# Regrouping the activations of a gated recurrence: the last three gates and the softplus exponential around the first gelu product

## The chip, the cores and the metric

The kernel runs on one core of a Trainium2 chip. The metric is the device time of one execution in microseconds (us). The engines that matter here are TensorE (PE, matrix products), VectorE (DVE, elementwise work, here also the scans), ScalarE (ACT, activation functions and copies with a scale) and SyncE (SP, which issues the loads). Each engine works through its own queue in order; the engines wait for each other through semaphores.

## The reference

One hybrid block over 16 meta tokens and 512 input tokens (528 rows of width 1024): a gated linear recurrence (RG-LRU) beside a retention branch, mixed, and then a convolutional feed-forward. The change touches the recurrence branch and, behind it, meets the projections of the retention branch:

```python
xr = causal_dwconv(u_rnn, rnn_conv_w, rnn_conv_b)
r = sigmoid(xb @ w_a + b_a)              # 10 blocks of 128 channels
i = sigmoid(xb @ w_x + b_x)
log_a = -8 * r * softplus(-lam)
a = exp(log_a)
b = sqrt(-expm1(2 * log_a)) * (i * x)
h_t = a_t * h_{t-1} + b_t                # scan over the tokens
o_a = h * gelu(u_gate)
...
q = rotary(xn @ w_q); k = rotary(xn @ w_k) / 16     # 4 heads of 256
```

## The kernel before, in words

**Data and tiles.** Tokens lie along the free axis, 128 channels on the partitions. Every fp32 operand of a large product is split in two fp16 parts, high (by ACT) and low (by DVE), and a product is the sum of three fp16 products: high·high, high·low, low·high (`SPLIT`, in that order of weight and input). The helper `split` (L92 on ACT, L93 on DVE) does this for weights and inputs alike. `project` (L401) makes one 128-channel product: eight steps of 128 input channels, in each step three fp16 products over two column halves, so 48 matmuls. In each step the low part of the weight is used last.

**Weights.** The weights come in numbered units of 1 MB (`unit`), 256 columns by 1024 input channels. SyncE loads a unit into one of two raw buffers (`raw`), in the order of the units; a load therefore waits until the split of the unit two before it is done. A unit of the plain kind is split in two halves, input channels 0 to 511 and 512 to 1023, so that the first half serves steps 1 to 4 of a product and the second half steps 5 to 8. One call of `tick` emits the split of one such half, as long as the tiles split but still ahead of the unit in use stay within `ahead`, here 6 tiles or three units. One unit serves two products. The units run on in this order: five for the recurrence input (`u_ur`), five for its gelu gate (`u_ug`), then query and key of each retention head in turn (`u_q[0]`, `u_k[0]`, `u_q[1]`, ...).

**Accumulators.** In the stage here `acc` gives out four PSUM tiles of two banks; a new product takes a free one and otherwise waits until the reader of an earlier one is done.

**Order.** Up to `order.close()` the program fixes the order on PE, ACT and DVE by hand: each of the three issues exactly in the order in which the program states its instructions. SyncE is left to the framework's planner. Behind `order.close()` everything is placed by the planner, which runs a model of the engines and at each moment issues the ready instruction with the highest priority (the earlier stated, the higher). It may also set instructions stated behind `order.close()` between those of the hand-written order, but cannot change that order itself.

**The recurrence.** For each of the ten blocks n the first loop makes the input product (`conv_product`), the convolution taps (`conv_taps`, L611 and L613) and the split `xs` of the result. Three blocks later (`LAG = 3`) `rnn_gates` makes the two gate projections (six matmuls each) and their sigmoids on ACT (L630), then multiplies the input gate in on DVE (L632). So blocks 7, 8 and 9 are still without gates when the first loop ends. Then the softplus of `lam` is worked out on ten columns: an absolute value and an exponential on ACT (L677, L678) and a short polynomial on DVE (L676 to L692), which ends in the scales `cneg` and `cpos`.

The second loop makes the ten products of the gelu branch. Round n is: the product (PE), one `tick` (one half of a weight, on ACT and DVE), the gelu on ACT (L702), in the first three rounds the gates of block 7 + n, and then what `SPREAD` lists for the round, for five blocks at once: `rnn_tanh` (ACT, L635), `rnn_decay` (exponential on ACT, L639, and two DVE instructions, L641 and L642), `rnn_scan` (square root on ACT, L646, a multiply and a scan on DVE, L647 and L648). Before, tanh stands in rounds 2 and 4, decay in 3 and 5, scan in 7 and 9. ACT evaluates its functions from a table that holds one set of them at a time; a function of another set brings an `ACT_TABLE_LOAD`. Abs, copy and identity bring none.

**Behind it.** `rotary` makes the two products of a query or key head (L401), whose weight halves are the ones split by the last ticks, and turns them on DVE (L742 to L744), with the tables `rope` that SyncE loads (L723). `branch_a` multiplies gelu and scan (L715).

Of the kernel before, what the change touches and what calls it, by code (L numbers as in the profile page):

```python
# [8 lines left out]
F32 = mybir.dt.float32  # L9
F16 = mybir.dt.float16  # L10
AF = mybir.ActivationFunctionType
ORDERED = {mybir.EngineType.PE, mybir.EngineType.Activation, mybir.EngineType.DVE}
ALU = mybir.AluOpType

P = 128
# [6 lines left out]
NR = DR // P  # L22
# [4 lines left out]
TQ = T - T0  # L27
# [3 lines left out]
SW = 2.0 ** 8  # L31
S_XN = 4.0
S_XR = 4.0
# [18 lines left out]
def hybrid_block_kernel(ctx, tc, x, meta, norm_mix_g, w_in, conv_w, conv_b, rg_a_w, rg_a_b,  # L52
                        rg_x_w, rg_x_b, lam, w_brnn, w_bret, w_out, norm_ffn_g, w_up,
                        fconv_w, fconv_b, w_down, norm_final_g, rope_t, decay_t, out):
    nc = tc.nc
    const = ctx.enter_context(tc.tile_pool(name="const", bufs=1))
# [17 lines left out]
    def acc(name):  # L74
        return psum["acc"].tile([P, 2, 512], F32, name=name, tag="acc")
# [9 lines left out]
    def piece(shape, dtype, name):  # L85
        return pieces.tile(shape, dtype, name=name, tag="s")

    def wtile(name):
        return work.tile([P, T], F32, name=name, tag="w")
# [198 lines left out]
    def get(u):  # L288
        current[0] = max(current[0], u)
        while len(loaded) <= u:  # L290
            queue(unit_load())
        while done[0] < len(steps) and steps[done[0]][0] <= u:
            emit_step()
        return wviews[u]

    def tick(n=1):

        for _ in range(n):
            if done[0] == len(steps):
                if len(loaded) == len(units):  # L300
                    return
                queue(unit_load())
            u = steps[done[0]][0]
            if sum(unit_tiles(i) for i in range(current[0], u + 1)) > ahead[0]:
                return
            emit_step()
# [10 lines left out]
    vt1 = const.tile([P, P], F32, name="vt1")  # L317
# [72 lines left out]
    def x_of(hi, lo):  # L390
        tv = (hi, lo)
        return lambda a, k, c0, n: tv[a][:, k, c0:c0 + n]
# [3 lines left out]
    def project(ps, w, col, src, halves, nk):  # L396

        for k in range(nk):
            for aw, ax in SPLIT:
                for hf, (c0, n) in enumerate(halves):  # L400
                    nc.tensor.matmul(ps[:, hf, :n], w(aw, k, col, P), src(ax, k, c0, n),  # L401
                                     start=k == 0 and (aw, ax) == (0, 0), stop=k == nk - 1 and aw == 1)
# [173 lines left out]
    half_r, half_t, half_x, gate_g = {}, {}, {}, {}  # L576

    def part(hv, n):
        if n not in hv:
            hv[n] = piece([P, T], F32, "rnn")  # L580
        return hv[n]
# [17 lines left out]
    def conv_product(n):  # L599
        u, col = u_ur[n]  # L600
        if n in early:
            ps = early.pop(n)
            project_half(ps, get(u), col, xf, HR, 1)
        else:
            ps = acc("ps")
            project(ps, get(u), col, xf, HR, KD)
        return ps
# [8 lines left out]
    def conv_split(n):  # L616
        xs = work.tile([P, 2, 1, T], F16, name="xs", tag="w")
        split(xs[:, 0, 0], xs[:, 1, 0], part(half_x, n), S_XR)
        xr_split[n] = xs

    def rnn_gates(n):
        xs = xr_split.pop(n)
        xr = part(half_x, n)
        gi = wtile("gi")
        for nm, bias, dst in (("a", b_a, part(half_r, n)), ("x", b_x, gi)):
            ps = acc("ps")
            wt = gw[nm][0][n // 4]
            project(ps, lambda a, k, c0, m: wt[:, a, n % 4 * P:n % 4 * P + P], 0, x_of(xs[:, 0], xs[:, 1]),
                    [(0, 264), (264, 264)], 1)
            nc.scalar.activation(dst.rearrange("p (a b) -> p a b", a=2), ps[:, :, :264], AF.Sigmoid,  # L630
                                 scale=1.0 / (SW * S_XR), bias=bias[:, n:n + 1])
        nc.vector.tensor_mul(xr, xr, gi)  # L632

    def rnn_tanh(n):
        nc.scalar.activation(part(half_t, n), part(half_r, n), AF.Tanh, scale=cpos[:, n:n + 1])  # L635
# [14 lines left out]
    LAG = 3  # L650
# [3 lines left out]
    for n in range(NR):  # L654
        ps = conv_product(n)
        if n == 0:
            split_gates("a")
        if n >= LAG:
            tick(2 if n in (4, 6, 8) else 1)
            rnn_gates(n - LAG)  # L660
        conv_taps(n, ps)
        if n == 0:
            conv_split(0)
        if n == 1:
            split_gates("x")
        if n == 2:
            tick()
            conv_split(1)
            psum_layout(acc=4)
        if n >= 2:  # L670
            conv_split(n)


    lv = vt1[:, 70:80]
    sp = const.tile([P, 8, NR], F32, name="sp")
    nc.vector.tensor_scalar(sp[:, 0], lv, -1.0, 0.0, op0=ALU.mult, op1=ALU.max)  # L676
    nc.scalar.activation(sp[:, 1], lv, AF.Abs)  # L677
    nc.scalar.activation(sp[:, 2], sp[:, 1], AF.Exp, scale=-1.0)  # L678
    nc.vector.tensor_scalar_add(sp[:, 3], sp[:, 2], 2.0)
    nc.vector.reciprocal(sp[:, 4], sp[:, 3])  # L680
    nc.vector.tensor_mul(sp[:, 4], sp[:, 4], sp[:, 2])
    nc.vector.tensor_mul(sp[:, 5], sp[:, 4], sp[:, 4])
    nc.vector.memset(sp[:, 6], 1.0 / 15.0)
    for m in (13, 11, 9, 7, 5, 3, 1):
        nc.vector.tensor_mul(sp[:, 6], sp[:, 6], sp[:, 5])
        nc.vector.tensor_scalar_add(sp[:, 6], sp[:, 6], 1.0 / m)
    nc.vector.tensor_mul(sp[:, 6], sp[:, 6], sp[:, 4])
    nc.vector.scalar_tensor_tensor(sp[:, 7], sp[:, 6], 2.0, sp[:, 0], op0=ALU.mult, op1=ALU.add)
    cneg = const.tile([P, NR], F32, name="cneg")
    cpos = const.tile([P, NR], F32, name="cpos")  # L690
    nc.vector.tensor_scalar_mul(cneg, sp[:, 7], -8.0)
    nc.vector.tensor_scalar_mul(cpos, sp[:, 7], 8.0)  # L692


    ahead[0] = 6
    SPREAD = ((rnn_tanh, 2, 0), (rnn_decay, 3, 0), (rnn_tanh, 4, 5), (rnn_decay, 5, 5), (rnn_scan, 7, 0), (rnn_scan, 9, 5))
    for n in range(NR):
        ps = acc("ps")
        u, col = u_ug[n // 2], (n % 2) * P
        project(ps, get(u), col, xf, HQ, KD)  # L700
        tick()
        nc.scalar.activation(part(gate_g, n)[:, :TQ].rearrange("p (a b) -> p a b", a=2), ps[:, :, :257],  # L702
                             AF.Gelu_apprx_tanh, scale=1.0 / (SW * S_XN))
        if n < LAG:
            rnn_gates(NR - LAG + n)
        for f, n0, m0 in SPREAD:
            if n == n0:
                for i in range(m0, m0 + 5):
                    f(i)
# [357 lines left out]
    def branch(us, src, nk):  # L1067
        ps = acc("pm")
        project(ps, get(us.pop(0)), 0, src, HH, nk)
        tick(2)  # L1070
        return ps[:, :, :257]
# [26 lines left out]
    for i in range(2):  # L1098
# [5 lines left out]
        ps = branch(u_ba, oa_of, NR)  # L1104
# [525 lines left out]
```

## Time and profile before

| | |
|---|---|
| Median of 3 runs | 1068.04 us (1067.8 to 1068.93) |
| The profiled execution's own time | 1068.13 us |
| Its span in the profile | 1066.4 us |
| PE busy | 1049.7 us (98%) |
| PE weight loads (PEld) busy | 851.7 us (80%) |
| DVE busy | 860.2 us (81%) |
| ACT busy | 589.1 us (55%) |
| Granted TensorE clock | 0.999 |

The profile is of one execution, with times from the start of its span; 1.7 us of the execution's own time lie outside the span. A row of a timeline gives start, duration, engine, line and operation, what is written and read with its shape, and the number of merged instructions; in brackets how long the engine was idle before it, and what released it. A row of a list of waits gives the total, the number of waits and the longest. L12 is line 12 of the kernel; as `split` and `project` are helpers, many groups share lines 92, 93 and 401, and are told apart by their tiles. The stage of the second loop lies between about 81 and 139 us, the products of the first query head behind it up to 149.5, those of the first key head up to about 160.6.

### The profile page before, as it was taken

The page shows a single profiled execution, that of the slowest core. Times are in us where ns is not written, and L with a number is a line of the kernel's source. Part 1 is how long each engine was busy: PE and PEld are TensorE (multiplying, and loading weights), DVE is VectorE, ACT ScalarE, POOL GpSimd, SP SyncE. Part 2 cuts the span into 40 slices and gives each one's busy share as a digit, 9 for nine tenths or more (in the row PEclk, how much of TensorE's full clock was granted, in tenths as well). Part 3 has the DMA queues.
Part 4 walks back from the last instruction along what each step waited for, and adds up shares of the span by engine and source line. Part 5 has one row for each costly group of instructions (what it writes and reads, how often), then busy time and mean ns, then how long its engine had stood idle before and what let it go on. Part 6 is the DMA issues. An engine that isn't in the chain of part 4 may idle for free.

```text
span 1066.4 us, 21008 instructions
## 1 busy us (share of the span) xinstructions
PE 1049.7 (98%) x8995; PEld 851.7 (80%) x8995; DVE 860.2 (81%) x1289; ACT 589.1 (55%) x927; POOL 6.9 (1%) x20
## 2 busy tenths in 40 slices
PE   9999999999999999999999999999999999999997
PEld 6888888865684848888888886588888888888884
DVE  6885799998786969887787886479989897988975
ACT  8568954434564747566454453366566465454442
POOL 2000000000000000000000000000000000000000
PEclk9999999999999999999999999999999999999999
DMA  8331243431211322333333365032432324214322
GB/s 255 102 133 45 80 139 119 160 120 40 78 43 47 113 65 65 115 94 109 115 110 115 105 221 179 1 119 80 159 111 88 120 81 136 64 60 137 102 80 80
DMA packets 108989, 111.49 MB, mean 105 GB/s; under 512 B 5610, under 2 KB 100560, under 8 KB 108896
## 3 DMA queue, kind: packets, MB, share of 16 engines
q1 hardware_dynamic: 108448, 109.74, 32.0%
q8 instruction: 70, 1.15, 0.4%
q10 hardware_dynamic: 160, 0.27, 0.1%
q0 software_dynamic: 288, 0.14, 0.1%
q14 instruction: 23, 0.19, 0.1%
HBM read 108.04 MB, written 2.10 MB: 103 GB/s over the span
## 4 chain that ended last, share of the span: by engine, by line
PE 78%; DVE 14%; ACT 6%; issue 2%; ACTq 0%; DVEq 0%
PE ps L401 31%; PE P L1466 9%; PE pa L852 9%; PE pm L401 4%; PE ps L915 4%; PE ps L1189 4%; PE pe L852 4%; DVE wt L93 3%; PE ps L414 3%; PE pb L852 2%; PE pa L1353 2%; ACT wt L92 2%; PE ps L937 1%; DVE rnn L648 1%; PE pe L1353 1%
## 5 line engine op out<-in xcount | busy, mean ns | idle before, releaser
L401 PEld LDWEIGHTS <-wt 128*128 128x128 f16 x3840 | 373.2, 97 | 58.2 <-DVE t L742 1.4
L93 DVE SCALAR_TENSOR_TENSOR wt<-raw,wt 128x1024 f16<-128x1024 f32 (+2 forms) x278 | 303.9, 1105 | 64.9 <-ACT wt L92 63.6
L92 ACT ACTIVATE wt<-raw 128x1024 f16<-128x1024 f32 (+2 forms) x278 | 263.4, 962 | 151.3 <-PE P L1466 25.3
L852 PEld LDWEIGHTS <-wt 128*128 128x128 f16 x2016 | 195.0, 97 | 34.7 <-issue 7.4
L401 PE MATMUL ps<-x2h,wt 128*128 128x258 f16 x1184 | 181.2, 273 | 0.0
L401 PE MATMUL ps<-xh,wt 128*128 128x257 f16 (+2 forms) x1056 | 163.8, 275 | 1.1 <-DVE t L742 1.1
L401 PE MATMUL ps<-x2l,wt 128*128 128x258 f16 x592 | 113.2, 272 | 0.0
L401 PE MATMUL ps<-xl,wt 128*128 128x257 f16 (+2 forms) x528 | 102.2, 275 | 0.0
L1466 PE MATMUL P<-wt,act 128*128 128x256 f16 x792 | 88.3, 273 | 0.0
L1466 PEld LDWEIGHTS <-act 128*128 128x128 f16 x792 | 77.5, 98 | 9.0
L915 PE MATMUL ps<-wt,xh 128*128 128x512 f16 x256 | 76.1, 379 | 2.3 <-DVE v L93 2.3
L1331 DVE SCALAR_TENSOR_TENSOR cv<-ps,vt,cv 128x512 f32<-128x512 f32 x80 | 59.7, 747 | 22.8 <-ACT cv L1329 21.9
L852 PE MATMUL pa<-xs,wt 128*128 128x257 f16 x576 | 71.6, 273 | 3.4 <-ACT kept L857 3.1
L401 PE MATMUL pm<-oa,wt 128*128 128x257 f16 x480 | 55.4, 274 | 0.0
L1329 ACT ACTIVATE cv<-ps,vt,vt 128x512 f32<-128x512 f32 x40 | 31.0, 774 | 34.5 <-PE ps L401 33.8
L915 PEld LDWEIGHTS <-xh 128*128 128x128 f16 x256 | 24.8, 98 | 31.4 <-issue 3.4
L915 PE MATMUL ps<-wt,xl 128*128 128x512 f16 x128 | 48.3, 379 | 0.0
L256 DVE TENSOR_TENSOR raw<-raw 128x1024 f32<-128x1024 f32 x39 | 47.6, 1220 | 0.7
L852 PE MATMUL pa<-ob,wt 128*128 128x257 f16 x384 | 45.7, 274 | 0.6 <-ACT last L857 0.5
L1189 PE MATMUL ps<-wt,mx 128*128 128x512 f16 x192 | 44.3, 378 | 0.0
L1353 PEld LDWEIGHTS <-wt 128*128 128x128 f16 x336 | 32.6, 97 | 4.4
L1189 PEld LDWEIGHTS <-mx 128*128 128x128 f16 x192 | 17.7, 98 | 18.4
(290 smaller groups left out, 1417.1 us busy)
## 6 DMA issues: line engine op xcount, KB each, us to landing
raw<-in_w_in SPq DMA_DIRECT2D x40, 1024.0 KB, 4.9
raw<-in_w_up SPq DMA_DIRECT2D x24, 1024.0 KB, 5.2
raw<-in_w_down SPq DMA_DIRECT2D x48, 256.0 KB, 3.5
raw<-in_w_branch_ret SPq DMA_DIRECT2D x16, 512.0 KB, 4.5
raw<-in_w_branch_rnn SPq DMA_DIRECT2D x8, 640.0 KB, 4.6
raw<-in_w_out SPq DMA_DIRECT2D x4, 1024.0 KB, 4.9
xin<-in_x SPq DMA_DIRECT2D x4, 512.0 KB, 5.5
raw<-in_w_in SPq DMA_DIRECT2D x4, 512.0 KB, 8.1
```

Source lines behind the costliest of these rows:

```text
L92: a = nc.scalar.activation(hi, src, AF.Copy, scale=s)
L93: b = nc.vector.scalar_tensor_tensor(lo, src, s, hi, op0=ALU.mult, op1=ALU.subtract)
L256: nc.vector.tensor_tensor(pair, pair, rv[:, :, right].rearrange("p (h k) c -> p h k c", h=2), op=ALU.add)
L401: nc.tensor.matmul(ps[:, hf, :n], w(aw, k, col, P), src(ax, k, c0, n), start=k == 0 and (aw, ax) == (0, 0), stop=k == nk - 1 and aw == 1)
L414: mm = nc.tensor.matmul(ps[:, hf, :n], w(aw, k, col, P), src(ax, k, c0, n), start=k == 0 and (aw, ax) == (0, 0), stop=k == KD - 1 and aw == 1)
L852: nc.tensor.matmul(ps[:, :257], ws[k // 4](wf, aw, k % 4), src(xf_, ax, k), start=first and k == 0 and (aw, ax) == (0, 0), stop=k == last_ ...
L915: nc.tensor.matmul(pb, xf(ax, k, XF + j0, nb), w(aw, k % 4, 0, 512), start=i == 0, stop=i == 23)
L1189: nc.tensor.matmul(ps[:, n], mx[k][:, a, c0:c0 + P], wo[k // 2](aw, k % 2, n * 512, 512), start=k == 0 and (a, aw) == (0, 0), stop=k == ks ...
L1329: nc.scalar.activation(vv_, src[:, :, 2:258], AF.Identity, scale=vt2[:, 96 + ch:97 + ch], bias=bias)
L1331: nc.vector.scalar_tensor_tensor(vv_, src[:, :, j:j + 256], vt2[:, 48 * j + ch:48 * j + ch + 1], vv_, op0=ALU.mult, op1=ALU.add)
L1353: nc.tensor.matmul(ps[:, :258], w(wf, aw, k), x2_form(xf_, ax, k), start=first and k == 0 and (aw, ax) == (0, 0), stop=k == 3 and aw == 1, ...
L1466: nc.tensor.matmul(pd[:, 256 * tt:256 * tt + 256], t[:, ax, c0 + tt * P:c0 + tt * P + P], w(wf, aw, i), start=q % 6 == 0 and tt == 0 and i ...
```

## The change

The gates of blocks 7, 8 and 9 are all stated in round 0, behind the product and the tick and ahead of its gelu. Behind them comes the softplus (now in a function `decay_scales`, unchanged inside), then the gelu of round 0. The gelus are also tied behind the last gate's sigmoid on ACT's queue (`tc.issue_after`), and so is the softplus' work on ACT. The two scan groups move from rounds 7 and 9 to 6 and 8.

```diff
@@ rnn_gates
-            nc.scalar.activation(dst.rearrange("p (a b) -> p a b", a=2), ps[:, :, :264], AF.Sigmoid,
-                                 scale=1.0 / (SW * S_XR), bias=bias[:, n:n + 1])
+            a = nc.scalar.activation(dst.rearrange("p (a b) -> p a b", a=2), ps[:, :, :264], AF.Sigmoid,
+                                     scale=1.0 / (SW * S_XR), bias=bias[:, n:n + 1])
         nc.vector.tensor_mul(xr, xr, gi)
+        return a.ins
...
+    def decay_scales():
         lv = vt1[:, 70:80]
         sp = const.tile([P, 8, NR], F32, name="sp")
...
         nc.vector.tensor_scalar_mul(cneg, sp[:, 7], -8.0)
         nc.vector.tensor_scalar_mul(cpos, sp[:, 7], 8.0)
+        return cneg, cpos

     ahead[0] = 6
-    SPREAD = ((rnn_tanh, 2, 0), (rnn_decay, 3, 0), (rnn_tanh, 4, 5), (rnn_decay, 5, 5), (rnn_scan, 7, 0), (rnn_scan, 9, 5))
+    SPREAD = ((rnn_tanh, 2, 0), (rnn_decay, 3, 0), (rnn_tanh, 4, 5), (rnn_decay, 5, 5), (rnn_scan, 6, 0), (rnn_scan, 8, 5))
     for n in range(NR):
         ps = acc("ps")
         u, col = u_ug[n // 2], (n % 2) * P
         project(ps, get(u), col, xf, HQ, KD)
         tick()
-        nc.scalar.activation(part(gate_g, n)[:, :TQ].rearrange("p (a b) -> p a b", a=2), ps[:, :, :257],
-                             AF.Gelu_apprx_tanh, scale=1.0 / (SW * S_XN))
-        if n < LAG:
-            rnn_gates(NR - LAG + n)
+        if n == 0:
+            for i in range(NR - LAG, NR):
+                gates_done = rnn_gates(i)
+            with tc.issue_after(gates_done):
+                cneg, cpos = decay_scales()
+        with tc.issue_after(gates_done):
+            nc.scalar.activation(part(gate_g, n)[:, :TQ].rearrange("p (a b) -> p a b", a=2), ps[:, :, :257],
+                                 AF.Gelu_apprx_tanh, scale=1.0 / (SW * S_XN))
         for f, n0, m0 in SPREAD:
             if n == n0:
                 for i in range(m0, m0 + 5):
                     f(i)
```

More of the change, by code (lines that the diff above doesn't have):

```diff
@@ L671, in hybrid_block_kernel @@
             conv_split(n)
[L674 to L691, printed above, removed]
@@ L692, in hybrid_block_kernel @@
-    nc.vector.tensor_scalar_mul(cpos, sp[:, 7], 8.0)
+    def decay_scales():
+        lv = vt1[:, 70:80]
+        sp = const.tile([P, 8, NR], F32, name="sp")
+        nc.vector.tensor_scalar(sp[:, 0], lv, -1.0, 0.0, op0=ALU.mult, op1=ALU.max)
+        nc.scalar.activation(sp[:, 1], lv, AF.Abs)
+        nc.scalar.activation(sp[:, 2], sp[:, 1], AF.Exp, scale=-1.0)
+        nc.vector.tensor_scalar_add(sp[:, 3], sp[:, 2], 2.0)
+        nc.vector.reciprocal(sp[:, 4], sp[:, 3])
+        nc.vector.tensor_mul(sp[:, 4], sp[:, 4], sp[:, 2])
+        nc.vector.tensor_mul(sp[:, 5], sp[:, 4], sp[:, 4])
+        nc.vector.memset(sp[:, 6], 1.0 / 15.0)
+        for m in (13, 11, 9, 7, 5, 3, 1):
+            nc.vector.tensor_mul(sp[:, 6], sp[:, 6], sp[:, 5])
+            nc.vector.tensor_scalar_add(sp[:, 6], sp[:, 6], 1.0 / m)
+        nc.vector.tensor_mul(sp[:, 6], sp[:, 6], sp[:, 4])
+        nc.vector.scalar_tensor_tensor(sp[:, 7], sp[:, 6], 2.0, sp[:, 0], op0=ALU.mult, op1=ALU.add)
+        cneg = const.tile([P, NR], F32, name="cneg")
+        cpos = const.tile([P, NR], F32, name="cpos")
+        nc.vector.tensor_scalar_mul(cneg, sp[:, 7], -8.0)
+        nc.vector.tensor_scalar_mul(cpos, sp[:, 7], 8.0)
+        return cneg, cpos
```

## The prediction

> **What bounds the kernel now.** I read the busy shares first, then what TensorE waits for, then the window of the changed stage engine by engine, then the chain that ended last.
>
> ```profile
> PE 1049.7 (98%) x8995; PEld 851.7 (80%) x8995; DVE 860.2 (81%) x1289; ACT 589.1 (55%) x927; POOL 6.9 (1%) x20
> ```
>
> ```profile
> 140.00:160.00 20.00, 20.00 (x180) 17.24 (x179) 20.00 (x23) 9.28 (x12) 0.00 (x0) 1.00 0.33 106
> ```
>
> ```profile
> 161.70 0.40 PE L401 MATMUL ps<-xh,wt 128*128 128x257 f16 x2 [1.12 <-DVE t L742]
> ```
>
> ```profile
> PE ps L915 <- DVE v L93: 2.3, 3, 1.5
> ```
>
> From top to bottom: busy time by engine; from the table by windows the stretch from 140 to 160 us, with the busy time of PE, the weight loads, DVE and ACT, and PE's granted clock third from the end; a row of TensorE's timeline; one of its list of waits. TensorE (PE) is busy for 1049.7 us, 98% of the span, so a gain can only come out of the other 2%, and any new idle time is a loss. From 140 to 160 us it has no gap; behind that stands one of 1.12 us, at 161.70: the first product of the second query head needs an accumulator, and all four are held by products of the first head, which VectorE (DVE) has not yet turned. DVE is full in this stretch (20.00 of 20.00), where ScalarE (ACT) is busy for less than half. Beyond this stage TensorE's largest waits on DVE are those of the value products, 2.3 us in three waits.
>
> ```profile
> 111.45 3.24 ACT rnn L639 x5
> ...
> 156.84 1.25 DVE rnn L648
> 161.70 65.04 PE ps L401 x576
> ```
>
> The chain of work that ended last passes through the exponentials on ScalarE, then DVE's scans, and returns to PE at 161.70. So ScalarE sets when DVE gets its decays and scans, and DVE sets that one gap.
>
> ```profile
> 90.03 0.60 ACT L702 ACTIVATE rnn<-ps 128x514 f32<-128x514 f32 x1
> ...
> 91.94 0.70 ACT L630 ACTIVATE rnn<-ps,vt 128x528 f32<-128x528 f32 x1
> ...
> 104.05 3.23 ACT L635 ACTIVATE rnn<-rnn,cpos 128x528 f32<-128x528 f32 x5
> 107.18 1.04 ACT L92 ACTIVATE wt<-raw 128x1024 f16<-128x1024 f32 x1
> 108.24 1.28 ACT L702 ACT_TABLE_LOAD   x1
> 109.53 0.60 ACT L702 ACTIVATE rnn<-ps 128x514 f32<-128x514 f32 x1
> 110.15 1.28 ACT L639 ACT_TABLE_LOAD   x1
> 111.45 3.24 ACT L639 ACTIVATE rnn<-rnn,cneg 128x528 f32<-128x528 f32 x5
> 114.59 1.04 ACT L92 ACTIVATE wt<-raw 128x1024 f16<-128x1024 f32 x1
> ...
> 116.95 0.60 ACT L702 ACTIVATE rnn<-ps 128x514 f32<-128x514 f32 x1
> 117.44 3.23 ACT L635 ACTIVATE rnn<-rnn,cpos 128x528 f32<-128x528 f32 x5
> ...
> 132.26 2.78 ACT L646 ACTIVATE rnn<-rnn 128x528 f32<-128x528 f32 x5
> ```
>
> On ScalarE's timeline, gelu, sigmoid, exponential and square root each bring a table load; tanh brings none behind sigmoid (104.05) or gelu (117.44). From start to start: gelu 0.62 ahead of a load and 0.49 else, load 1.29, five tanh 3.13, five exponentials 3.14, a weight split 1.06 ahead of a load. Where no load follows, the next record starts 0.1 ahead of the end (gelu lasts 0.60), so that split counts 0.95.
>
> **The change, part by part.** *The gates.* Six projections move behind the first gelu product; PE's work is the same, and the product n=3 still starts at 101.47.
>
> ```profile
> 100.12 1.51 PE L401 MATMUL ps<-xs,gw 128*128 128x264 f16 x12
> 101.47 0.39 PE L401 MATMUL ps<-xh,wt 128*128 128x257 f16 x2
> ```
>
> The pair of gate projections takes 1.35, 0.67 for each. The first product keeps its accumulator, since its gelu now stands behind the sigmoids; three are free. The fourth projection needs the first one's accumulator 1.35 after that projection ended; its sigmoid takes 0.70 (row 91.94 with no load: the sigmoid set is still active) and some 0.2 to start. It is free 0.4 in time, so I cost this at nothing; the cover is that margin. The two loads per gate pair go; with the sequence gelu, sigmoid, gelu undone, and with the scans' square roots at n=6 and 8, I count ten loads instead of fifteen.
>
> *The softplus.*
>
> ```profile
> 87.80 0.17 DVE L679 TENSOR_SCALAR sp<-sp 128x10 f32<-128x10 f32 x1 [0.83 <-ACT sp L678]
> ...
> 92.05 0.17 DVE L692 TENSOR_SCALAR cpos<-sp 128x10 f32<-128x10 f32 x1
> ```
>
> Of its instructions on DVE those behind the exponential take 4.3 us, and move to some 93.3 to 97.7 us, behind the last sigmoid, the load and the exponential. Queued behind them are one weight split and, on SyncE, the load that waits for that split's buffer, some 3 us later than now. What it brings is not split before the fifth round, at 112 by the sum below, and the tanh that needs the softplus starts at 102.2: nothing.
>
> *ScalarE's path.* The third gelu starts when its product has ended, 101.67. Then 0.49 + 3.13 (tanh) + 0.95 (split) gives 106.24; the fourth gelu waits for its product until 107.0; 0.62 + 1.30 leads to the exponentials at 108.92 (before: 111.45). Then 3.14 + 1.06 + 1.29 + 0.49 gives tanh at 114.91; 3.13 + 0.95 + 0.61 + 1.29 exponentials at 120.89; 3.14 + 1.06 + 1.29 + 0.62 + 1.29 the first square root at 128.3 (before 132.26). From gelu to sigmoid, 90.03 to 91.94 is 1.91, where gelu to tanh is 0.49: a switch costs 1.42 here.
> The Trainium skill (ScalarE: Activation LUTs, What ACT_TABLE_LOAD costs) gives 2.66 us for a switch, 1283 ns and a drain of 1380 ns. The load's 1283 ns agrees with the trace, the whole switch does not; by that figure the five loads ahead of the first square root would put it an estimated 6 us later, and the wait worked out below would be that much longer. I go by the rows.
>
> *DVE's path.* Here the moved scans matter most.
>
> ```profile
> 112.22 0.71 DVE L641 TENSOR_TENSOR a<-rnn 128x528 f32<-128x528 f32 x1 [2.73 <-ACT rnn L639]
> ...
> 119.03 1.22 DVE L93 SCALAR_TENSOR_TENSOR wt<-raw,wt 128x1024 f16<-128x1024 f32 x1
> ...
> 130.99 2.35 DVE L93 SCALAR_TENSOR_TENSOR wt<-raw,wt 128x1024 f16<-128x1024 f32 x2
> 133.26 0.70 DVE L647 TENSOR_TENSOR rnn<-rnn 128x528 f32<-128x528 f32 x1
> ...
> 135.17 0.69 DVE L647 TENSOR_TENSOR rnn<-rnn 128x528 f32<-128x528 f32 x1
> 135.77 0.69 DVE L715 TENSOR_TENSOR rnn<-rnn 128x514 f32<-128x514 f32 x1
> ...
> 137.54 0.68 DVE L647 TENSOR_TENSOR rnn<-rnn 128x528 f32<-128x528 f32 x1
> ...
> 145.19 2.33 DVE L93 SCALAR_TENSOR_TENSOR wt<-raw,wt 128x1024 f16<-128x1024 f32 x2
> ...
> 160.37 0.67 DVE L744 TENSOR_TENSOR t<-t,t 128x514 f32<-128x514 f32 x1
> ```
>
> DVE follows ScalarE's exponential by 0.77 (111.45 to 112.22), and ten decay instructions take 6.81, up to the split at 119.03. After: 120.89 + 0.77 + 6.81 = 128.5. In the code a tick (one weight split) stands in each round ahead of the scans. Before, both halves of the first query head's weight (row 130.99, 2.27 for two) precede the first five scans, and both halves of the first key head's weight (row 145.19) precede the last five. With the scans one round earlier, the second half of each falls behind its five scans, in an order that DVE may not change. Step by step: query half 1 ends 128.5 + 1.14 = 129.6; then the scans begin. Before, from 133.26 to 160.37 (27.1 us) DVE did ten scan pairs, nine other instructions that were put between a multiply and its scan, and the two key halves. After, the same stretch has query half 2 as well (1.14), less 0.54 because one of the inserted weight splits cannot be loaded yet: it ends at 129.6 + 27.1 + 1.1 - 0.5 = 157.3, and the last thing in it is now the second half of the key weight. Before, that half was done at 147.5. Query half 2 comes after five scans: 1.91 for the first pair, 2.37 for each with an inserted instruction, 129.6 + 11.4 + 1.14 = 142.2.
>
> *The loads behind it.*
>
> ```profile
> 133.79 1.05 SPq L723 DMA_DIRECT2D rope<-rope  x2
> 147.59 51.36 SPq L104 DMA_DIRECT2D raw<-in_w_in  x8
> ```
>
> ```profile
> raw<-in_w_in SPq DMA_DIRECT2D x40, 1024.0 KB, 4.9
> ```
>
> On SyncE's queue the load for the second query head, with the two rotary tables right behind it (133.79), waits for query half 2's buffer, and those at 147.59 for the key half's. They move to 142.2 and 157.4. At 4.9 us to landing the first is there at 147 and the next at 162; PE needs the second key head's weight some 10 us after the second query head has begun, at 172. Split times of 2 us included, the loads cost nothing. The rotary tables land near 148, ahead of most of the turning.
>
> *What PE then meets.*
>
> ```profile
> 138.58 0.61 PE L401 MATMUL ps<-xh,wt 128*128 128x257 f16 x4
> ...
> 149.25 0.61 PE L401 MATMUL ps<-xh,wt 128*128 128x257 f16 x4
> ```
>
> Each row has two matmuls that end a product and two that begin the next, so the query head's two products take from 138.8 to 149.5, 5.34 each, and the key head's first starts at 149.5. The query product needs the low part of half 2 in its fifth of eight steps, at 138.8 + 2.67 + 0.45 = 141.9: a wait of 0.3. The key product's steps are 0.68 (264 columns instead of 257), so it needs the low part of half 2 at 149.5 + 2.74 + 0.46 = 152.7, while DVE delivers at about 157.4. That is a new wait of 4.7 us if PE has nothing else.
> It does have something else: the other product of the same head, whose first four steps need only half 1 and for which an accumulator is free. Whether they are put there is decided by the planner, since these products lie outside the hand-written order.
>
> ```profile
> 229.97 0.22 PE L787 MATMUL ps<-qk,krep 128*128 128x16 f16 x3
> 230.05 0.59 PE L915 MATMUL ps<-wt,xh 128*128 128x512 f16 x2
> ...
> 230.88 0.23 PE L787 MATMUL ps<-qk,krep 128*128 128x16 f16 x3
> ```
>
> Here it did such a thing: three score matmuls, then three of the value product, then three scores again. With the second product's first half and its first four high matmuls in the gap (2.74 + 0.46), PE runs until 155.9 and waits 1.5; the 0.3 at the query product is covered in the same way. I take this value.
>
> *The sum.* The gap of 1.12 at 161.70 goes: behind the scans, DVE frees accumulators from about 159, ahead of PE. New wait 1.5. Net +0.4 on the profiled execution's 1068.13 us, which is 0.09 over the median of the runs (1068.04): 1068.5. The bounds of the unknown: with nothing inserted between multiply and scan (1.91 for each pair) the stretch ends at 129.6 + 19.1 + 3.4 = 152.1, and PE waits for nothing, -1.1; with nothing put into PE's gap the wait is 4.7 + 0.3, net +3.9. I stand nearer to the filled gap because of the rows at 229.97 to 230.88. The later, smaller waits I leave as they are.
>
> **The rivals.**
> *Unfilled gap, slower.* The planner keeps PE's products in order at 152.7 and PE idles until DVE ends the tenth scan and key half 2. It decides from 155.6 us on (152.7 plus 1.1 + 2.1 us, less the 0.3 at the query). For it: project's matmuls of one product stand together everywhere else in the rotary stage. Against it: the interleaved rows at 230. Time: 1068.13 + 3.9 = 1072.0.
> The trace shows no TensorE wait in this stage longer than 1.12, and a clock of 1.00 throughout.
> By the Trainium skill (TensorE: Matmul & The Clock Gate, HAM oscillation) an idle gap over some 3.4 us lets the clock fall to half until TensorE has been busy as long again; that would add an estimated 1.7 us to this rival. No run here shows such a gap.
>
> *DVE early enough.* Fewer instructions are inserted, or the planner's order gives the scans way sooner, and key half 2 is done by 155.9. For it: DVE starts the scans 133.26 - 129.6 = 3.6 earlier. Against: nine of ten pairs had an insertion before, and the gated products are there to insert sooner still. Then only the 1.12 goes: 1067.0.
>
> *The lead carries on.* With DVE full from 140 us on, its lead could last to the value stage and shorten the waits on it there, 2.3 us. For it: they end with a split on DVE. Against: the row has three waits, the longest of 1.5, so they look like local meetings of two queues more than a backlog. Time: 1068.13 - 1.1 - 2.3 = 1064.7 if all of them go.
>
> **How the numbers follow.** Filled gap 0.42 (1067.6 to 1069.6), unfilled 0.28 (1070.3 to 1073), DVE early enough 0.20 (1066.2 to 1067.4), lead carries on 0.10. About 0.2%, 2.1 us, is what a measurement of this kernel can tell from no change. Slower than that: nearly all of the unfilled gap, 0.27; faster: the carried lead, 0.10; within: 0.63. The range leaves out the ends of the first and last, 1066.0 to 1072.2. No case here is a mishap of the table loads: if their number did not fall, ScalarE would be as late as before and the scans would still stand ahead of the splits, which falls into the unfilled case.
>
> **What would show it.** In the profile after: ten table loads between 85 and 145 us instead of fifteen; first exponential at 108.9, first root at 128.3; DVE's first scan near 130.4; the wait at 161.70 gone; a weight split as DVE's last instruction after the tenth scan, near 157, and a TensorE or weight-load wait on it between 152 and 158. If PE runs through 140 to 160 us without a gap, my DVE path or the order is wrong; if PE waits in the 87 to 91 us stretch, the accumulator margin is.

## The result, and the profile after

The changed kernel takes 1075.99 us (median of 5 runs, 1075.39 to 1077.07) against 1068.04 (5 runs, 1067.8 to 1068.93): 1.0075 times the time before, 95% interval 1.0064 to 1.0085. It is 8.0 us slower; the forecast was 1068.5 with a range up to 1072.2. The profiled execution took 1076.03 us, with a span of 1074.3 and a mean granted clock of 0.995.

The busy times, first line of the page after (compare 1049.7, 860.2 and 589.1 before):

```profile
PE 1051.6 (98%) x8995; PEld 852.5 (79%) x8995; DVE 860.5 (80%) x1289; ACT 584.6 (54%) x923; POOL 6.9 (1%) x20
```

TensorE does the same 8995 matmuls and is busy 1.9 us longer: some of them ran slower. The rest of the 8 us must be new idle time. ScalarE's timeline after, the rows that the prediction had dated (start, duration, operation):

```profile
101.44 0.60 ACT L712 ACTIVATE rnn<-ps 128x514 f32<-128x514 f32 x1 [3.79 <-PE ps L401]
...
108.69 3.24 ACT L640 ACTIVATE rnn<-rnn,cneg 128x528 f32<-128x528 f32 x5
...
114.68 3.22 ACT L636 ACTIVATE rnn<-rnn,cpos 128x528 f32<-128x528 f32 x5
...
120.65 3.24 ACT L640 ACTIVATE rnn<-rnn,cneg 128x528 f32<-128x528 f32 x5
...
128.06 2.78 ACT L647 ACTIVATE rnn<-rnn 128x528 f32<-128x528 f32 x5
```

The first exponentials start 2.76 us earlier than before (111.45), the first square root 4.20 earlier (132.26). On DVE's timeline the scans follow at once, and the second halves of the weights stand behind them:

```profile
129.37 0.70 DVE L648 TENSOR_TENSOR rnn<-rnn 128x528 f32<-128x528 f32 x1
130.11 1.26 DVE L649 TENSOR_TENSOR_SCAN rnn<-rnn 128x528 f32<-128x528 f32 x1
...
140.77 2.33 DVE L93 SCALAR_TENSOR_TENSOR wt<-raw,wt 128x1024 f16<-128x1024 f32 x2
...
154.79 1.25 DVE L649 TENSOR_TENSOR_SCAN rnn<-rnn 128x528 f32<-128x528 f32 x1
155.96 1.20 DVE L93 SCALAR_TENSOR_TENSOR wt<-raw,wt 128x1024 f16<-128x1024 f32 x1
```

The row at 140.77 is the second half of the query weight and the first of the key weight; that at 155.96 is the second half of the key weight, directly behind the tenth scan. TensorE's timeline and its list of waits show who needed it:

```profile
142.02 0.62 PE L401 MATMUL ps<-xh,wt 128*128 128x257 f16 x4 [0.17 <-DVE wt L93]
...
152.57 0.39 PE L401 MATMUL ps<-xl,wt 128*128 128x264 f16 x2
157.21 1.06 PE L401 MATMUL ps<-xh,wt 128*128 128x264 f16 x4 [4.25 <-DVE wt L93]
...
161.15 1.05 PE L401 MATMUL ps<-xh,wt 128*128 128x264 f16 x4
162.03 0.40 PE L401 MATMUL ps<-xl,wt 128*128 128x264 f16 x2
162.27 0.62 PE L401 MATMUL ps<-xh,wt 128*128 128x264 f16 x4
...
251.54 1.05 PE L915 MATMUL ps<-wt,xlast 128*32 128x512 f16 x16
...
293.56 7.57 PE L945 MATMUL ps<-sc,v 128*128 128x257 f16 x96 [2.11 <-DVE sf L802]
```

```profile
PE ps L401 <- DVE wt L93: 4.4, 2, 4.3
...
PE ps L945 <- DVE sf L802: 2.1, 1, 2.1
```

Three things are new. TensorE idles for 4.25 us ahead of 157.21, in the middle of the first key head's first product. Behind that gap four matmuls last 1.06, where four of the same shape last 0.62 at 162.27. And at 293.56, far from the change, the first retention product (the decayed scores of head 0 times its values, L945) waits 2.11 us for an instruction of DVE that multiplies scores by their decay (`sf`, the score factors), which it did not do before. The 1.12 at 161.70 is gone. Windows of the kernel after, placed on the clock's changes (length; busy PE, weight loads, DVE, ACT, POOL; then the granted clock, third from the end):

```profile
148.38:151.79 3.41, 3.41 (x33) 2.93 (x31) 3.41 (x5) 0.53 (x1) 0.00 (x0) 1.00 0.00 0
151.79:155.21 3.42, 1.17 (x11) 0.76 (x8) 3.42 (x5) 0.00 (x0) 0.00 (x0) 1.00 0.00 0
155.21:158.62 3.41, 1.41 (x7) 1.00 (x8) 3.41 (x5) 0.00 (x0) 0.00 (x0) 0.50 0.78 256
158.62:162.03 3.41, 3.41 (x17) 2.32 (x16) 3.41 (x6) 2.16 (x3) 0.00 (x0) 0.50 1.09 348
162.03:165.45 3.42, 3.42 (x31) 2.92 (x30) 3.42 (x6) 2.67 (x5) 0.00 (x0) 1.00 0.04 11
...
291.74:295.15 3.41, 1.58 (x18) 1.43 (x18) 3.41 (x10) 1.27 (x4) 0.00 (x0) 1.00 0.15 58
```

From 155.21 to 162.03 TensorE has half its clock. From 157.21 to 162.03 it makes 22 matmuls in 4.82 us; at the full clock six of them take 0.685, so 22 take 2.51. The half clock costs 2.3 us.

The account can be checked at two landmarks, a product of 16 matmuls in the value stage and the first retention product. Before, on TensorE's timeline:

```profile
245.95 1.05 PE L907 MATMUL ps<-wt,xlast 128*32 128x512 f16 x16
...
285.72 7.67 PE L937 MATMUL ps<-sc,v 128*128 128x257 f16 x96
```

The first is 5.59 us later after (251.54), the second 7.84 (293.56). 4.25 + 0.17 + 2.3 - 1.12 is 5.6, and the 2.11 makes it 7.7. Five terms so explain the 8 us. That the 5.6 meets the 5.59 so closely is partly luck, as two small things nearly cancel: the execution after is already 0.22 us ahead at 30 us, ahead of the changed stage, and a wait costs some 0.16 more from start to start than the idle time in its row (from 152.57 to 157.21 is 4.64, of which two matmuls take 0.22; the row says 4.25).

### The profile page after: what moved, and what is told of

Its sections match the earlier page's. It is cut to its first block, busy times and chain, and to the rows that moved or that the text cites. A ratio compares the mean times of both kernels' runs of the same rounds, so it can differ in the third digit from the quotient of the medians.

```text
span 1074.3 us, 21012 instructions
## 1 busy us (share of the span) xinstructions
PE 1051.6 (98%) x8995; PEld 852.5 (79%) x8995; DVE 860.5 (80%) x1289; ACT 584.6 (54%) x923; POOL 6.9 (1%) x20
## 4 chain that ended last, share of the span: by engine, by line
PE 79%; DVE 15%; ACT 3%; issue 2%; DMA 0%; DVEq 0%; ACTq 0%
PE ps L401 34%; PE P L1474 9%; PE pa L860 9%; PE pm L401 4%; PE ps L923 4%; PE ps L1197 4%; PE pe L860 4%; DVE wt L93 3%; PE ps L414 3%; PE pb L860 2%; PE pa L1361 2%; ACT wt L92 1%; PE ps L945 1%; DVE rnn L649 1%; PE pe L1361 1%
## 5 line engine op out<-in xcount | busy, mean ns | idle before, releaser
L945 PE MATMUL ps<-sc,v 128*128 128x257 f16 (+4 forms) x384 | 32.1, 236 | 2.1 <-DVE sf L802 2.1
```

What stands on the lines that cost most here:

```text
L945: nc.tensor.matmul(ps[:, hf, s0 - lo_i:257], vt[b][:, va, d * P:(d + 1) * P], st[SCP[b][0]][:, sa, o:o + hi_i - s0], start=i == 0, stop=i ...
```

## The theories and the experiments

Theory A: the earlier place of the scans puts each second weight half behind five scans on DVE; TensorE waits for them, and its clock falls in the wait. The gates, gelus and softplus by themselves gain. The rival to it is that the regrouped gates or the load on DVE delay the stage. The wait at 293 us was in neither; theory B on it follows below, behind the first four experiments. The experiments were timed in three groups, each on one chip beside the kernel before (1067.92 us in the first group, the four up to bare_scans; 1067.94 in the third, before_rotated and gates_rotated_2; 1068.05 in the second, the others).

**gates_only.** The change, with the scans back in their old rounds.

```diff
-    SPREAD = (... (rnn_scan, 6, 0), (rnn_scan, 8, 5))
+    SPREAD = (... (rnn_scan, 7, 0), (rnn_scan, 9, 5))
```

> The changed kernel with the scans put back into rounds 7 and 9; the regrouped gates, softplus and gelus stay. Theory A (the loss comes from the scans' place alone: in rounds 6 and 8 they push the second weight half of the query and of the key head behind them on DVE): both halves are split ahead of their scans again, TensorE waits nowhere between 85 and 200 us, and the 1.12 us at 161.70 goes since the scans begin near 130.9 instead of 133.3: 1067.0 us. If the new 2.1 us wait of the first retention product stays all the same: 1069.1. Rival B (the loss comes from the regrouped gates, the accumulator kept longer or the weight split that the softplus delays): about 1075, with the waits where they are in the changed kernel.

Measured: 1070.81 us (1069.37 to 1072.14, 7 runs), ratio 1.0025 (1.0014 to 1.0036). TensorE's timeline:

```profile
244.87 1.05 PE L915 MATMUL ps<-wt,xlast 128*32 128x512 f16 x16
...
286.89 7.57 PE L945 MATMUL ps<-sc,v 128*128 128x257 f16 x96 [2.11 <-DVE sf L802]
```

and DVE's, the instruction for which it waits:

```profile
286.67 0.16 DVE L802 SCALAR_TENSOR_TENSOR sf<-ps,dec_meta 128x16 f32<-128x16 f32 x1
```

Up to 244.87 there is no wait on a weight half, the half clock is gone, and the kernel is 1.08 us ahead of before (245.95). That is about the 1.12 at 161.70, regained; 0.20 of lead that this execution had already at 30 us and a new wait of 0.22 ahead of 192.91 cancel each other. Then comes the 2.11, here too. So the gap at 157 us comes from the scans, and the later wait from the gates, not from a late DVE: the same instruction of DVE starts at 287.76 before, 1.09 later than here. The profiled execution took 1069.42, near the 1069.1 expected with the wait; most of the others took 1 to 3 us longer, to which the last section comes back.

**scans_only.** The kernel before, with nothing but the scans one round earlier.

```diff
-    SPREAD = (... (rnn_scan, 7, 0), (rnn_scan, 9, 5))
+    SPREAD = (... (rnn_scan, 6, 0), (rnn_scan, 8, 5))
```

> The kernel before with nothing changed but the scans in rounds 6 and 8. Theory A: the same order on DVE as in the changed kernel, but ScalarE is later (first root near 130.8), so the scans begin near 132.2 and key half 2 is done near 159.9: TensorE waits some 7 us in all between 141 and 160, the clock falls to half for some 6.8 us (2.3 us lost), the 1.12 goes: 1076.4, or 1078.5 with the retention wait of 2.1. Rival B: 1068, as before.

Measured: 1075.38 us (1074.17 to 1076.12, 4 runs), ratio 1.0069 (1.0054 to 1.0084). TensorE's timeline at its two waits, and windows:

```profile
144.47 0.62 PE L401 MATMUL ps<-xh,wt 128*128 128x257 f16 x4 [2.70 <-DVE wt L93]
159.66 1.06 PE L401 MATMUL ps<-xh,wt 128*128 128x264 f16 x4 [2.61 <-DVE wt L93]
```

```profile
142.14:145.55 3.41, 1.07 (x10) 0.95 (x11) 3.41 (x4) 2.36 (x3) 0.00 (x0) 1.00 0.02 2
145.55:148.97 3.42, 3.42 (x18) 2.40 (x17) 3.42 (x6) 0.00 (x0) 0.00 (x0) 0.50 0.99 327
...
155.79:159.20 3.41, 1.26 (x12) 0.84 (x9) 3.41 (x4) 0.00 (x0) 0.00 (x0) 1.00 0.19 42
159.20:162.62 3.42, 2.96 (x14) 2.00 (x15) 3.42 (x7) 0.57 (x2) 0.00 (x0) 0.50 1.08 367
```

ScalarE is not ahead here, so both second halves are late, by 2.70 and 2.61. Each wait brings one stretch of 3.41 us at half the clock, which costs half of TensorE's busy time in it: 1.71 and 1.48. 5.31 + 3.19 - 1.12 is 7.4, and 7.5 was measured. The scans' place alone, with the gates left as they were, makes a loss of this size. There is no 2.11 at the retention product.

**halves_first.** The change, with both halves of a weight ahead of each scan group.

```diff
-        tick()
+        tick(2 if n in (6, 8) else 1)
```

> The changed kernel with two ticks in rounds 6 and 8 instead of one, so that both halves of the query weight and both of the key weight are split ahead of the scans, which stay in rounds 6 and 8. Theory A: no wait at 142 and 153, clock 1.00, scans from 130.6: 1067.0, or 1069.1 with the retention wait. Rival B: about 1075. Rival C (the early scans themselves, not the order of the halves, hold TensorE up): above 1073.

Measured: 1071.38 us (1069.65 to 1072.75, 6 runs), ratio 1.003 (1.0017 to 1.0043). There is no wait from 140 to 160 us, and one of 0.96 on a weight split at 171.89. What stays is the retention product, and in the profiled execution the clock fell there:

```profile
287.48 9.15 PE L945 MATMUL ps<-sc,v 128*128 128x257 f16 x96 [2.11 <-DVE sf L802]
```

9.15 for the 96 matmuls instead of 7.57: 1.6 us more. With the scans left early and only the halves put ahead of them, the gap is gone, so the order on DVE is the cause.

**bare_scans.** The change, with the gated branch's multiplies tied behind the last hand-ordered weight split, so that none of them can be put between a multiply and its scan.

```diff
...
+    scans_end = last_split[0]
...
     def branch_a(n):
+      with tc.issue_after(scans_end):
```

> The changed kernel with the gelu-times-scan products tied behind the last weight half of the hand-written order on DVE, so that nothing stands between a multiply and its scan. Theory A: each scan pair takes 1.91 instead of 2.4 to 2.9, key half 2 is done at 129.4 + 19.1 + 3.4 = 151.9, just ahead of TensorE's 152.9: no wait, clock 1.00: 1067.0, or 1069.1 with the retention wait. If the inserted instructions cost nothing (DVE's pace set by the scans alone): still 157 and 1076.

Measured: 1072.32 us (1070.74 to 1072.48, 4 runs), ratio 1.0038 (1.0023 to 1.0053). One row of TensorE's waits, one of its timeline:

```profile
PE ps L403 <- DVE t L754: 1.6, 3, 0.8
```

```profile
288.63 9.15 PE L949 MATMUL ps<-sc,v 128*128 128x257 f16 x96 [2.11 <-DVE sf L806]
```

The scans run denser and no wait on a weight half is left, but the turning of the heads (`t`) becomes late: 1.6 us in three waits from 160 us on. With the 1.6 that the fall of the clock costs at the retention product, this makes up the 3.2 by which the time is above the 1069.1 expected. The inserted multiplies were part of the 4.25, as the prediction's lower bound had it, and have to be done all the same.

**Theory B.** The wait of 2.11 is in every kernel with the regrouped gates, and not in scans_only. DVE's timeline, the last score factors ahead of it, those of head 3, before and then after:

```profile
287.76 0.16 DVE L794 SCALAR_TENSOR_TENSOR sf<-ps,dec_meta 128x16 f32<-128x16 f32 x1
```

```profile
293.35 0.16 DVE L802 SCALAR_TENSOR_TENSOR sf<-ps,dec_meta 128x16 f32<-128x16 f32 x1
```

Before, the retention product starts 2.0 us ahead of this instruction (285.72); after, right behind it (293.56). So it does not need this instruction's result to start (it is the product of head 0, and the factors are head 3's); what it can need from it is the PSUM that the instruction reads. The scores of a head come in three groups, each in an accumulator of its own. The compiled programs give the banks of the accumulators, by their number in the program:

```
                       score groups of head 3      first retention product
                       first   second  third
before                 bank 0  bank 2  bank 6      bank 0
after                  bank 6  bank 4  bank 0      bank 0
```

The accumulators are taken in turn. The regrouped gates change the turn, which runs on through the rotary and value stages. Then the pool is laid out anew, two accumulators instead of four, and the first one lies on banks 0 and 1: before, these were last read for the first score group, after, for the third. Theory B: that alone is the wait. Its rival is that DVE is later there for some other reason.

**fill_by_hand.** The change, with TensorE's order for the first key head stated.

```diff
...
+            for k0 in (0, 4):
+                for m in range(2):
+                    some_steps(pp[m], wv, m * P, xf, halves, range(k0, k0 + 4))
...
```

> The kernel after the change, with the order of the first key head's two products stated: the first four steps of both, then the last four of both. If the missing work in the gap is the cause (theory A), TensorE has 2.74 us of the second product and 0.46 of high matmuls to do while the second half of the weight is split: the wait of 4.25 falls to about 1.1, the clock stays at 1.00 from 150 to 165 us, and the time is 1076.0 - 3.2 - 2.3 = 1070.5. If the fall of the clock does not hang on the idle time (rival), the granted clock still drops near 155 us and the time is 1072.8. The wait of 2.1 us of the first retention product stays in either case.

Measured: 1071.35 us (1070.72 to 1072.36, 5 runs), ratio 1.0034 (1.0022 to 1.0046).

```profile
157.70 0.63 PE L409 MATMUL ps<-xh,wt 128*128 128x264 f16 x4 [1.51 <-DVE wt L93]
...
288.98 7.57 PE L960 MATMUL ps<-sc,v 128*128 128x257 f16 x96 [2.11 <-DVE sf L817]
```

```profile
157.00:158.00 1.00, 0.30 (x3) 0.27 (x4) 1.00 (x2) 0.00 (x0) 0.00 (x0) 1.00 1.01 353
158.00:160.00 2.00, 2.00 (x20) 1.70 (x19) 2.00 (x5) 0.00 (x0) 0.00 (x0) 1.00 1.08 365
```

The wait is 1.51 and not 1.1: the 4.25 already has the high matmuls of the fifth step behind it (TensorE was idle from 152.96), so only 2.74 can be taken off. With the gap short, the clock stays at 1.00. This is the filling on which the prediction stood, less the second product's four high matmuls of its fifth step (0.46). That the wait is the 1.5 that it gave is partly luck: TensorE runs out at 155.7 and not 155.9, and DVE delivers at 157.2 and not 157.4.

**busy_gap.** The change, with 24 matmuls of the first key product made twice.

```diff
+            if u == u_k[0] and m == 0:
+                for k in range(4):
...
+                            nc.tensor.matmul(ps[:, hf, :w], wv(aw, k, 0, P), xf(ax, k, c, w), ...)
```

> The kernel after the change, with the first four steps of the first key head's first product made twice (24 matmuls, 2.74 us of work that serves nothing), so that TensorE is busy for most of the gap without anything being gained from it. Theory A, in which the idle time itself lets the clock fall: wait 1.5 instead of 4.25, clock 1.00 throughout the stage, and only the clock's loss comes back: 1076.0 - 2.3 = 1073.7. Rival, in which the clock's fall costs nothing or comes from something else: 1076.0, with a clock of about 0.5 behind 155 us as before.

Measured: 1074.95 us (1074.88 to 1075.05, 4 runs), ratio 1.0065 (1.0052 to 1.0079).

```profile
157.17 0.63 PE L401 MATMUL ps<-xh,wt 128*128 128x264 f16 x4 [1.51 <-DVE wt L93]
...
291.19 9.15 PE L951 MATMUL ps<-sc,v 128*128 128x257 f16 x96 [2.10 <-DVE sf L808]
```

```profile
158.00:160.00 2.00, 2.00 (x20) 1.72 (x18) 2.00 (x4) 0.00 (x0) 0.00 (x0) 1.00 1.08 356
```

Work that serves nothing makes this kernel 1.0 us faster than the change. The clock stays at 1.00 behind the gap, which gives back 2.3; at the retention product it fell in the profiled execution, which takes 1.6 (9.15 instead of 7.57). That fall, at a new place, accounts for the 1.2 by which the time is above the 1073.7 expected.

**after_rotated.** The change, and one additional accumulator in each of three rounds, so that bank 0 goes to the first score group of head 3 again.

```diff
+        if n in (1, 2, 3):
+            spare = acc("spare")
+            nc.vector.memset(spare[:, 0, 0:2], 0.0)
```

> The kernel after the change, with one more accumulator taken in each of the rounds 1, 2 and 3 (two columns of it are written by VectorE, nothing reads them), so that the accumulators stand on the same banks behind the stage as in the kernel before. Theory B, in which the regrouped gates shift that rotation and the first retention product has to wait for the banks of the last score group instead of the first: the wait of 2.11 at 293.6 us goes, the gap at 157 us and its fall of the clock stay, time 1073.9 (1072.3 if a second fall of the clock goes with it). Rival, in which VectorE is simply later there: the wait stays at 2.1 and the time at 1076.0.

Measured: 1073.3 us (1073.1 to 1073.77, 4 runs), ratio 1.0051 (1.0035 to 1.0066).

```profile
157.00 1.06 PE L401 MATMUL ps<-xh,wt 128*128 128x264 f16 x4 [4.26 <-DVE wt L93]
...
291.05 7.57 PE L948 MATMUL ps<-sc,v 128*128 128x257 f16 x96
```

The gap and its half clock are there as before, and the wait of 2.11 is gone.

**before_rotated.** The kernel before with the same three lines, nothing of the change.

> The kernel before, with nothing of the change, and the three additional accumulators of the rounds 1, 2 and 3 alone. Here they do the opposite of what they do in the kernel after: they put the first retention accumulator on the banks that the last score group of its head held. Theory B: a wait of 2.1 us of the first retention product on VectorE's score factors appears near 286 us, time 1068.0 + 2.1 = 1070.1, or 1071.7 in executions in which the clock falls with it. The clock should fall, by the ten profiles so far, where 2.07 us or more of the idle time lie within one of the 3.413 us steps counted from the clock's first rise, and not where 1.83 us or less do. Rival, in which that wait comes from the regrouped gates or from VectorE's load: no such wait, 1068.0 to 1068.3.

Measured: 1073.28 us (1071.44 to 1073.51, 4 runs), ratio 1.0045 (1.003 to 1.006). Timeline, and windows on the clock's steps:

```profile
95.35 0.38 PE L401 MATMUL ps<-xh,wt 128*128 128x257 f16 x2 [0.60 <-DVE spare L704]
...
289.29 9.15 PE L940 MATMUL ps<-sc,v 128*128 128x257 f16 x96 [2.11 <-DVE sf L797]
```

```profile
286.35:289.76 3.41, 1.30 (x21) 1.15 (x20) 3.41 (x10) 2.03 (x6) 0.00 (x0) 1.00 0.58 226
289.76:293.18 3.42, 3.42 (x28) 2.64 (x26) 1.26 (x4) 0.67 (x2) 0.00 (x0) 0.50 0.43 139
```

The same lines that take the wait from the kernel after bring it to the kernel before. Theory B holds: banks, not load. The time is above the 1070.1 to 1071.7 expected, by the 0.60 that TensorE waits for a spare accumulator at 95.35, by a new wait of 0.29 on a turned head at 184 us, and by some 0.7 us that are not traced.

**gates_rotated, gates_rotated_2.** gates_only with the same three lines, run twice.

> Regrouped gates, scans back in rounds 7 and 9, and the same additional accumulators. If theories A and B hold together, neither the gap at 157 us nor the wait of 2.11 at 293 us is there, the clock stays near 1.00, and the gain of 1.1 us that the regrouped gates had up to 247 us is kept to the end: 1067.0 (1066.6 to 1067.5), below the kernel before, with no more scatter than that has. If the 2.11 comes from VectorE's order and not from the banks, the time stays at 1069.4 to 1072.1, as without the additional accumulators.

> The same kernel as gates_rotated once more, to narrow its interval: 1067.2 again, 0.9 us below the kernel before. If the first result was chance, the ratio moves to 1.000 or above.

Measured: 1067.16 us (1067.12 to 1067.7, 11 runs) and 1067.2 (1067.13 to 1067.66, 11 runs), ratio 0.9993 both times (0.9984 to 1.0002 and 0.9985 to 1.0002).

```profile
284.55 7.57 PE L948 MATMUL ps<-sc,v 128*128 128x257 f16 x96
```

No wait stands ahead of the retention product, 1.17 us earlier than before. The intervals still reach past 1, but the slowest of the second 11 runs (1067.66) is below the fastest of the 15 runs of before beside them (1067.82). What the regrouped gates are worth is some 0.8 us by the medians; in the change as made, the 2.1 us of the banks and the 6.7 of the scans' place (4.25, 0.17 and 2.3) stand against it.

## Why the prediction was wrong

*The gates, the softplus:* right. The list of waits has no accumulator wait in the gates' stretch.

*ScalarE's path:* right. The five dates were 101.67, 108.92, 114.91, 120.89 and 128.3; the rows say 101.44, 108.69, 114.68, 120.65 and 128.06, all 0.23 or 0.24 earlier, as the whole execution is at that point. There are ten table loads. The rows' 1.42 for a switch is borne out. By the 2.66 of the Trainium skill (ScalarE: Activation LUTs, What ACT_TABLE_LOAD costs) the first root would have come an estimated 6 us later; the trace does not agree with that.

*DVE's path:* right. The second query half was to be done at 142.2 and was at 142.0, the second key half at 157.3 (157.4 in the lines on PE) and was at 157.2.

*The loads behind it:* right, no further weight wait.

*What PE then meets:* the sums were right within 0.5 us (0.3 and 4.7; found 0.17 and 4.25), and the choice behind them wrong. I took it that the planner would put the second product's first half into the gap, from three interleaved rows of the value stage. It kept the two products in order, and TensorE idled from 152.96; the 0.17 at the query product was not covered either. This is the step that failed first: a wait of 4.25 where 1.5 stood in the sum. fill_by_hand shows that the work could be done there, takes 2.74 off the wait, and keeps the clock at 1.00. It still takes 1071.35, so this step alone does not explain the miss. Why the planner interleaves at 230 us and not at 153 was not tried and stays open.

*The clock:* it stood only in a sentence on the Trainium skill beside the rival, 1.7 us, and in no sum. It is a term of 2.3 us here, and hangs on the gap being left unfilled. The Trainium skill (TensorE: Matmul & The Clock Gate, HAM oscillation) names a gap of over some 3.4 us as the condition; in this case 2.1 us of idle time were enough (below).

*"The later, smaller waits I leave as they are":* wrong by 2.11, the accumulators' turn. I asked whether the moved projections would find a free accumulator, and not which banks the later ones would then get.

The rival *Unfilled gap, slower* was the right mechanism and gave 1072.0; with its own waits (-1.12 + 4.25 + 0.17 = +3.3), the clock's 2.3 and the banks' 2.1 the sum is 1068.1 + 7.7 = 1075.8. *DVE early enough* fell with the 157.2. *The lead carries on* fell too: the value products' waits are 2.3 us in three waits in every kernel here.

## What to carry to other kernels

When a group is moved forward in a queue with a fixed order, look for what stood ahead of it and now stands behind: here a 1.2 us weight split behind 13 us of scans, on which another engine waits. Price a new TensorE wait of 2 us or more with the half clock that can follow it (1.5 to 2.3 us here), and don't count on a planner to fill it unless the trace shows it filling that very place. Regrouping work that takes buffers in turn can shift every later buffer: compare the bank assignments of the two programs up to the next change of layout.

## What the runs showed of the hardware

The granted clock changes in steps. In all twelve profiles, counted from the clock's first rise, every fall and every rise lies at a whole multiple of 3.413 us (44 and 46 in the kernel after, 83 and 84 in before_rotated), and that first rise lies anywhere from 4.5 to 7.5 us behind the span's start. What goes with a fall is TensorE's idle time within one such step. From the first rise up to the last stage, in which TensorE runs out of work, the steps at full clock with 2.07 to 2.34 us of it (eight, in seven kernels) are each followed by a step at half the clock, and none of the others, with up to 1.83, is. Nothing between 1.83 and 2.07 was met. A step with 2.01 us that was itself at half the clock (155.21 in the kernel after) did not end it; a step full of work did.

So one and the same wait of 2.11 us costs 2.1 or 3.7 us: in the kernel after it fell across two steps (1.83 in the row 291.74:295.15), in before_rotated into one. That it differs between executions of one kernel is not shown, as only the profiled ones show the clock's steps, but the mean clock of every execution points that way: of the four of bare_scans three took 1072.2 to 1072.5 us at 0.997 and one 1070.74 at 0.999, and of the four of before_rotated three took 1073.2 to 1073.5 at 0.997 and one 1071.44 at 0.999. It may so be a part of why gates_only scatters over 2.8 us and gates_rotated, without the wait, over 0.6; one fall's 1.6 is not all of that. The expectation for before_rotated was written by this rule, and its profile agrees. The Trainium skill (TensorE: Matmul & The Clock Gate, What's actually happening) describes a window of 3413 ns that runs free of the kernel's start. The trace agrees with that; that the whole window must be idle, it does not bear out.
